# A transformer block in split fp32 on one core: w_down by seven products over pairs of column blocks

## The chip, the cores and the metric

The kernel runs on one core of one Trainium2 chip. The metric is the device time of one execution in microseconds, the median of several runs. A profile is one more execution, recorded by the hardware profiler; its span runs from the first to the last instruction.

## The reference

One layer for 256 tokens of width 2048, all in float32:

```python
h = x + concat(diff_attention(...), conformer_conv(...)) @ w_out     # from rms_norm(x) @ w_in
hn = rms_norm(h, norm2_g)
a  = hn @ w_gate          # 2048 x 5632
bu = hn @ w_up            # 2048 x 5632
y  = h + (silu(a) * bu) @ w_down    # 5632 x 2048
```

The change lies in the last line.

## The kernel before

**Split products.** A float32 product is made of three matmuls in a rounded format: each operand is cut into a hi half (rounded) and a lo half (what rounding left), and hi x hi, lo x hi and hi x lo are added up in a PSUM bank. A weight tile `raw` is loaded by SP's queue; ACT casts it to `whi`; DVE subtracts to get `wlo` (`split_chunk`, L326). For chunks with `by_dma`, ACT writes minus the hi half into `wlo` (L320) and a DMA on POOL's queue adds the weight from DRAM to it (L321), so DVE is spared.

**Chunks.** All matrix products are a list of chunks, run in order by `run_chunks`. Each chunk is loaded, rounded, split and multiplied, with leads (how many chunks ahead of the multiplication) given by the function `lead`: (5, 5, 3, 2) for load, DMA, hi and lo in the gate blocks, 2 for everything in the rest. What ends (a block's sums) runs as a generator, `start`ed at the end of a block and `resume`d twice in a chunk, so its steps land between the steps of the chunks that follow, in program order, on each engine. Engines take their instructions in that order.

**The feed-forward part.** The hidden width 5632 is cut into eleven blocks j of 512 columns of w_gate and w_up. They form three groups (`FGROUPS = (4, 4, 3)`); after each group w_down is applied to that group's columns (the w_down stage of groups 0, 1 and 2).

Blocks 1 to 10 are fast blocks: gate and up for both halves of the tokens form a 2x2 by 2x2 product, done with seven products in place of eight (Strassen's scheme in Winograd's form) on four pairs of k-tiles, and plainly on the other eight k-tiles. An "s" unit is one pair of k-tiles: ACT rounds the raw tiles `wb` to `wh` (L910), DVE makes three sums of weights `wt` (L907 to L909), ACT rounds these too (L911), DVE makes `wl` (L915 from wb, L916 from wt), and PE makes 7 products x 3 matmuls (L932 to L934), added to the banks Q1 to Q7. A "g" or "u" unit is a two: two k-tiles of gate or up, plain, 12 matmuls (L949, L950, L955). The order of the units is a string, with a capital where the lo half is made by DMA:

```python
ORDER = "sgGsgGsUUsUu"   # blocks 2 to 10
FIRST = "gugusgsUsGsU"   # block 1
PRODUCTS = ((Q1, 0, 5), (Q6, 5, 1), (Q7, 6, 2), (Q5, 4, 3), (Q2, 1, 6), (Q4, 3, 0), (Q3, 2, 4))   # bank, form of hn, form of the weights
```

A fast block is 4 x 21 + 8 x 12 = 180 matmuls of 128x512. When its last s unit is done, `products_done` copies bank Q1 on ACT and adds up the other banks on DVE; after the block's last unit, `block_done` adds the last two banks, multiplies by silu of the gate (L1013, L1015), and some chunks later `transposed` turns the result into left operands for w_down: two sets of four transposes on PE (`ps_a`, L827), each turned into `ahi` by ACT (L829) and `alo` by DVE (L831).

The w_down stage of a group has four column blocks of 512, each with 16 (12 in group 2) k-tiles x 2 token halves x 3 matmuls (L356, L357, L362), in chunks of two k-tiles: 384 matmuls (288). Groups 0 and 1 copy each result from PSUM on ACT (`part`) and add it to the output in DRAM with a DMA on POOL's queue. Group 2 fetches the sums so far over SP's queue (`fetch_sums`, L1025), adds on DVE and writes the result.

Of the kernel before, what the change touches and what calls it, by code (L numbers as in the profile page):

```python
# [18 lines left out]
P = 128  # L19
D = 2048  # L20
# [37 lines left out]
RAW_BUFS = 5  # L58
# [24 lines left out]
PRODUCTS = ((Q1, 0, 5), (Q6, 5, 1), (Q7, 6, 2), (Q5, 4, 3), (Q2, 1, 6), (Q4, 3, 0), (Q3, 2, 4))  # L83

LOAD_AHEAD, DMA_AHEAD, HI_AHEAD, LO_AHEAD = 5, 5, 3, 2

# [14 lines left out]
def tile_block(  # L101
# [9 lines left out]
    small = ctx.enter_context(tc.tile_pool(name="small", bufs=4))  # L111

    lhs = ctx.enter_context(tc.tile_pool(name="lhs", bufs=KD // 2))
# [3 lines left out]
    pre = prestack.enter_context(tc.tile_pool(name="pre", bufs=2))  # L117
    acc_ps = ctx.enter_context(tc.tile_pool(name="acc", bufs=4, space=PSUM))
# [22 lines left out]
    cols = const.tile([P, NR], F32, tag="cols", name="cols")  # L141
# [11 lines left out]
    neg_lam = const.tile([P, 1], F32, tag="neg_lam", name="neg_lam")  # L153
# [55 lines left out]

    halves = {}  # L210
# [6 lines left out]
    def lhs_two(pfx, k):  # L217
        return tuple(lhs.tile([P, 2, S], F32R, tag=f"l{x}", name=f"{pfx}{x}{k}") for x in ("hi", "lo"))
# [165 lines left out]
    def run_chunks():  # L384
# [16 lines left out]
        for t in range(n):  # L401
# [17 lines left out]
            if t in fetch_at:  # L419
                fetch_sums(fetch_at[t])  # L420
# [8 lines left out]
    rstd1 = [const.tile([P, 1], F32, tag=f"rstd1_{m}", name=f"rstd1_{m}") for m in range(NM)]  # L429
# [324 lines left out]
    ss2 = [const.tile([P, 4], F32, tag=f"ss2_{m}", name=f"ss2_{m}") for m in range(NM)]  # L754
    rstd2 = [const.tile([P, 1], F32, tag=f"rstd2_{m}", name=f"rstd2_{m}") for m in range(NM)]

    def out_done(n, ps):
# [28 lines left out]
        if n == D // N - 1:  # L786
# [8 lines left out]
            ffn["pool"] = ctx.enter_context(tc.tile_pool(name="ffn", bufs=1))  # L795
# [23 lines left out]

    def transposed(j, aa):  # L820
        for t in range(N // P // 2):
# [6 lines left out]
            hi, lo = lhs_two("a", j * (N // P) + 2 * t)  # L828
            act.copy(hi, pt)  # L829
            yield from lag(2)  # L830
            dve.tensor_tensor(lo, pt, hi.bitcast(F32), ALU.subtract)  # L831
            for i in range(2):
                actT[j * (N // P) + 2 * t + i] = (hi[:, i, :], lo[:, i, :])
            yield from lag(2 if j else 1)

    forms = {}

    def make_forms():  # L840
# [33 lines left out]
        f = fp.tile([P, 7, NS, P], F32, tag="wh", name="sums", bufs=2)  # L874
        dve.scalar_tensor_tensor(f[:, 4], a21, -1.0, a22, ALU.mult, ALU.subtract)
        dve.scalar_tensor_tensor(f[:, 5], f[:, 4], -1.0, a11, ALU.mult, ALU.subtract)
        act.copy(fhi[:, 0], a11)
        act.copy(fhi[:, 1], a12)
        act.activation(fhi[:, 3], a22, AF.Copy, scale=-1.0)
        yield  # L880
        dve.tensor_tensor(f[:, 6], a11, a21, ALU.subtract)
        dve.tensor_tensor(f[:, 2], a12, f[:, 5], ALU.subtract)
        act.copy(fhi[:, 4:7], f[:, 4:7])
        act.copy(fhi[:, 2], f[:, 2])
# [4 lines left out]
        dve.scalar_tensor_tensor(flo[:, 3], a22, -1.0, fhi[:, 3].bitcast(F32), ALU.mult, ALU.subtract)  # L889
        dve.tensor_tensor(flo[:, 2], f[:, 2], fhi[:, 2].bitcast(F32), ALU.subtract)  # L890
        yield
        dve.tensor_tensor(flo[:, 4:7], f[:, 4:7], fhi[:, 4:7].bitcast(F32), ALU.subtract)
        forms.update(hi=fhi, lo=flo)

    def load_pair(c):
        c["b"] = early.tile([P, 4, N], F32, tag="wb", name="wb")
        src = weights([(w, k, c["col"], N) for w in ("w_up", "w_gate") for k in (c["k"], c["k"] + HK)])
        sp.dma_start(out=c["b"].rearrange("p k n -> p (k n)"), in_=src)
# [26 lines left out]
    def multiply_pair(c):  # L925
        while "hi" not in forms:
            resume()
        fhi, flo, p = forms["hi"], forms["lo"], c["k"]
        for n, (q, f, w) in enumerate(c["products"]):
# [11 lines left out]
    def multiply_two(c):  # L941
        hi, lo = c["hi"], c["lo"]
        qs = (Q3, QX) if c["kind"] == "u" else (Q2, Q4)
        for i, k in enumerate(c["ks"]):
            x1, x2 = forms["plain"][k]
            for m, q in enumerate(qs):
                ms = slice(m * P, (m + 1) * P)
                ps = sum_bank(c, q)
                pe.matmul(ps, x1[:, ms], hi[:, i, :], start=i == 0 and bool(c["first"].get(q)), stop=False)  # L949
                pe.matmul(ps, x2[:, ms], hi[:, i, :], start=False, stop=False)  # L950
        resume()
        for m, q in enumerate(qs):
            ms = slice(m * P, (m + 1) * P)
            for i, k in enumerate(c["ks"]):
                pe.matmul(sum_bank(c, q), forms["plain"][k][0][:, ms], lo[:, i, :], start=False,  # L955
                          stop=i == 1 and bool(c["last"].get(q)))
# [4 lines left out]
    def fast_block(j, order, after_down):  # L961

        units, sums = [], {}
        left = dict(s=list(range(NS)), g=list(TWOS), u=list(TWOS))
        for unit in order:
            kind = unit.lower()
            what = left[kind].pop(0)
            c = dict(kind=kind, sums=sums, done=None, first={}, last={})
            if kind == "s":
                c.update(k=what, col=j * N, by_dma=False, load=load_pair, round=round_pair, split=split_pair,  # L970
                         multiply=multiply_pair, uses=[q for q, _, _ in PRODUCTS], products=PRODUCTS)
            else:
                c.update(ks=what, w="w_gate" if kind == "g" else "w_up", nk=2, width=N, cols=[(j * N, N)],
                         by_dma=unit.isupper(),
                         load=load_chunk, round=round_chunk, split=split_chunk, multiply=multiply_two,
                         uses=(Q3, QX) if kind == "u" else (Q2, Q4))
            units.append(c)
        assert not any(left.values())
        if after_down:

            units[0]["products"] = PRODUCTS[4:] + PRODUCTS[:4]
        for q in range(8):
            users = [c for c in units if q in c["uses"]]
            users[0]["first"][q] = users[-1]["last"][q] = True
        [c for c in units if c["kind"] == "s"][-1]["done"] = products_done
        units[-1].update(done=lambda sums: block_done(j, sums), prompt=True)
        chunks.extend(units)
# [3 lines left out]
    def products_done(q):  # L991
# [11 lines left out]
        act.activation(w1, w1, AF.Silu)  # L1003
        dve.tensor_tensor(u3, q[Q4], u3, ALU.add)
        act.activation(u3, u3, AF.Silu)
        halfway.update(g=(w1, u3), u=(u2, w4))

# [11 lines left out]
    so_far, fetch_at = {}, {}  # L1019

    def fetch_sums(n):
        so_far[n] = []
        for m in range(NM):
            t = ffn["pool"].tile([P, N], F32, tag=f"sum{n % 2 * NM + m}", name="so_far")
            sp.dma_start(out=t, in_=out[m * P : (m + 1) * P, n * N : (n + 1) * N])  # L1025
# [102 lines left out]
```

## Time and profile before

| | |
|---|---|
| median of 3 runs | 1081.86 us (1079.11 to 1083.89) |
| profiled execution, its own time | 1078.51 us |
| its span | 1076.7 us |
| gate blocks 1, 2, 3 | 397.8 to 526.1 us |
| w_down stage of group 0 | 526.1 to 614.1 us |
| gate blocks 4 to 7 | 614.1 to 783.2 us |
| w_down stage of group 1 | 783.2 to 871.2 us |
| gate blocks 8 to 10 | 871.2 to 997.7 us |
| w_down stage of group 2 | 997.7 to 1072.1 us |

Engines: PE is TensorE's matmul, PEld its weight load, DVE VectorE, ACT ScalarE, POOL GpSimd, SP SyncE. L12 is line 12 of the kernel. A row of instructions gives start and duration, then what was written and read; in brackets, the idle time before it and what ended it. A matmul's recorded duration overlaps the next one's, so matmuls are priced by the distance of their starts. A suffix q (SPq) is an engine's queue that issues DMAs.

### The profile page before, as it was taken

What the parts mean: (1) busy time and instruction counts of PE and PEld (TensorE: products, weight loads), DVE (VectorE), ACT (ScalarE), POOL (GpSimd) and SP (SyncE); (2) the same over time, 40 slices, a digit from 0 to 9 for tenths busy, and PEclk for the clock granted to TensorE, in tenths of its full rate; (3) what the DMA queues carried; (4) which work ended last, traced back from release to release, by engine and by line L of the source; (5) the groups of instructions that cost most, each with busy time, mean ns of one, the idle gap of its engine ahead of it and who ended that gap; (6) DMA issues with size and microseconds to landing.
All of it is one profiled execution on the core that took longest, in us unless ns stands there. A gap on an engine that the chain in (4) does not pass through costs nothing. (4 is left out here: it accounts for less than half of the span.)

```text
span 1076.7 us, 13151 instructions
## 1 busy us (share of the span) xinstructions
PE 1051.7 (98%) x4834; PEld 870.9 (81%) x4834; DVE 801.4 (74%) x979; ACT 618.0 (57%) x811; POOL 110.4 (10%) x155
## 2 busy tenths in 40 slices
PE   8999999999999999999999999999999999999798
PEld 7988888877888887788888878878888878888686
DVE  4799988899666689988644688889745477897353
ACT  6544566756756557757343667586544474765231
POOL 0130112200100100101000111010001010100000
PEclk9999999999999999999999999999999999999899
DMA  9555555344457568898476898988847799887471
GB/s 314 205 176 180 200 189 176 137 176 151 143 190 242 175 228 252 284 304 244 153 232 197 267 295 252 293 221 268 259 157 201 239 277 319 223 273 208 145 278 66
DMA packets 62781, 236.57 MB, mean 220 GB/s; under 512 B 7044, under 2 KB 8510, under 8 KB 57596
## 3 DMA queue, kind: packets, MB, share of 16 engines
q1 hardware_dynamic: 52320, 202.66, 52.1%
q0 software_dynamic: 10336, 33.04, 16.6%
q8 instruction: 38, 0.62, 0.2%
q14 instruction: 27, 0.22, 0.1%
q10 hardware_dynamic: 60, 0.03, 0.0%
HBM read 227.30 MB, written 8.39 MB: 219 GB/s over the span
## 5 line engine op out<-in xcount | busy, mean ns | idle before, releaser
L317 ACT CAST whi<-raw 128x1024 fp32r<-128x1024 f32 (+1 forms) x297 | 305.8, 1050 | 183.2 <-PE acc L357 98.1
L326 DVE TENSOR_TENSOR wlo<-raw,whi 128x1024 fp32r<-128x1024 f32 (+1 forms) x249 | 299.7, 1219 | 142.8 <-ACT whi L317 140.9
L357 PE MATMUL acc<-whi,alo 128*128 128x512 f32 x384 | 150.5, 392 | 6.6 <-DVE alo L831 6.6
L356 PE MATMUL acc<-whi,ahi 128*128 128x512 f32 x384 | 150.4, 392 | 0.0
L356 PE MATMUL acc<-whi,xhi 128*128 128x512 f32 (+1 forms) x352 | 131.0, 378 | 3.2 <-ACT xhi L223 2.4
L357 PE MATMUL acc<-whi,xlo 128*128 128x512 f32 (+1 forms) x352 | 129.5, 374 | 0.5 <-DVE xlo L224 0.4
L949 PE MATMUL q<-whi,chi 128*128 128x512 f32 x320 | 124.7, 390 | 0.0
L950 PE MATMUL q<-whi,clo 128*128 128x512 f32 x320 | 124.6, 389 | 0.0
L932 PE MATMUL q<-wh,fhi 128*128 128x512 f32 x280 | 109.7, 392 | 1.7 <-DVE alo L831 1.7
L934 PE MATMUL q<-wl,fhi 128*128 128x512 f32 x280 | 109.0, 389 | 0.0
L933 PE MATMUL q<-wh,flo 128*128 128x512 f32 x280 | 109.0, 389 | 0.0
L512 DVE SCALAR_TENSOR_TENSOR y<-upad,cw,y 128x256 f32<-128x256 f32 x240 | 103.7, 483 | 4.4 <-ACT y L505 3.9
L362 PE MATMUL acc<-wlo,ahi 128*128 128x512 f32 x384 | 103.6, 391 | 0.0
L911 ACT CAST wh<-wt 128x2048 fp32r<-128x2048 f32 x40 | 76.5, 1912 | 38.3 <-DVE wt L909 37.6
L916 DVE TENSOR_TENSOR wl<-wt,wh 128x2048 fp32r<-128x2048 f32 x40 | 91.7, 2291 | 6.6 <-ACT wh L911 5.9
L915 DVE TENSOR_TENSOR wl<-wb,wh 128x1536 fp32r<-128x1536 f32 x40 | 70.1, 1754 | 27.9 <-ACT wh L910 27.9
L357 PEld LDWEIGHTS acc<-whi,alo 128*128 128x128 f32 x384 | 72.6, 189 | 22.1 <-DVE alo L831 6.9
L362 PE MATMUL acc<-wlo,xhi 128*128 128x512 f32 (+1 forms) x352 | 88.3, 376 | 1.4 <-DVE wlo L326 1.4
L955 PE MATMUL q<-wlo,chi 128*128 128x512 f32 x320 | 86.6, 392 | 2.8 <-DMA wlo<-in_wts_dram 2.8
L356 PEld LDWEIGHTS acc<-whi,ahi 128*128 128x128 f32 x384 | 72.5, 189 | 15.3 <-ACT ahi L829 0.2
L362 PEld LDWEIGHTS acc<-wlo,ahi 128*128 128x128 f32 x384 | 71.7, 188 | 14.6
L356 PEld LDWEIGHTS acc<-whi,xhi 128*128 128x128 f32 x352 | 67.2, 191 | 14.9 <-ACT xhi L223 2.8
(197 smaller groups left out, 1487.2 us busy)
## 6 DMA issues: line engine op xcount, KB each, us to landing
raw<-in_wts_dram SPq DMA_DIRECT2D x295, 512.0 KB, 4.9
wb<-in_wts_dram SPq DMA_DIRECT2D x40, 1024.0 KB, 6.2
wlo<-in_wts_dram POOLq DMA_DIRECT2D x48, 512.0 KB, 8.3
out_dram<-part POOLq DMA_DIRECT2D x16, 256.0 KB, 5.1
out_dram<-h POOLq DMA_DIRECT2D x8, 256.0 KB, 5.9
so_far<-out_dram SPq DMA_DIRECT2D x8, 256.0 KB, 4.4
h<-in_x_dram SPq DMA_DIRECT2D x6, 256.0 KB, 7.6
out_dram<-so_far POOLq DMA_DIRECT2D x6, 256.0 KB, 3.0
```

What stands on the lines that cost most here:

```text
L317: act.copy(c["hi"], c["raw"])
L326: dve.tensor_tensor(c["lo"], c["raw"], c["hi"].bitcast(F32), ALU.subtract)
L356: pe.matmul(ps[m], xhi[:, ms], hi[:, j, :], start=c["first"] and j == 0, stop=False)
L357: pe.matmul(ps[m], xlo[:, ms], hi[:, j, :], start=False, stop=False)
L362: pe.matmul(ps[m], xhi[:, ms], lo[:, j, :], start=False, stop=c["last"] and j == nk - 1)
L512: dve.scalar_tensor_tensor(y[:, ct, :], src, wk, y[:, ct, :], ALU.mult, ALU.add)
L916: dve.tensor_tensor(c["lo"][:, :4], c["t"], c["hi"][:, :4].bitcast(F32), ALU.subtract)
L932: pe.matmul(ps, fhi[:, f, p, :], c["hi"][:, w], start=bool(first), stop=False)
L933: pe.matmul(ps, flo[:, f, p, :], c["hi"][:, w], start=False, stop=False)
L934: pe.matmul(ps, fhi[:, f, p, :], c["lo"][:, w], start=False, stop=bool(last))
L949: pe.matmul(ps, x1[:, ms], hi[:, i, :], start=i == 0 and bool(c["first"].get(q)), stop=False)
L950: pe.matmul(ps, x2[:, ms], hi[:, i, :], start=False, stop=False)
```

## The change

w_down now uses `fast_block` too. Two neighbouring column blocks take the place of up and gate; three pairs of the group's k-tiles go through the seven products, the remaining five twos (three in group 2) are plain. A block of two column blocks is 3 x 21 + 10 x 12 = 183 matmuls where there were 192, in group 2 63 + 6 x 12 = 135 where there were 144; there are two such blocks in a group.

- The three pairs of each group need seven forms of the left operand, hi and lo: `pair_forms` makes them when the tile is transposed, that is in the next gate block: two pairs in blocks 2, 5 and 9, one in 3, 6 and 10. A plain tile is treated as before.
- The bank sums are one step, all on DVE, with the copy of Q1; sums of the second column block go to DRAM (POOL's queue) as soon as the products are done, those of the first when the block is.
- PRODUCTS has another order: the first product reads a form from the second half of wl (the one made of wt).
- Leads are 5, 5, 3, 2 from the first gate block to the end. The first block after a w_down stage no longer starts with other products.
- The lo half of four of ten twos (two of six in group 2) in a w_down block is made by DMA.
- Only the last block fetches sums, on POOL's queue. RAW_BUFS is 4 instead of 5. The left operands lie in one `arena`; small tiles of the earlier stages are closed earlier.

```diff
-RAW_BUFS = 5
+RAW_BUFS = 4
-PRODUCTS = ((Q1, 0, 5), (Q6, 5, 1), (Q7, 6, 2), (Q5, 4, 3), (Q2, 1, 6), (Q4, 3, 0), (Q3, 2, 4))
+PRODUCTS = ((Q6, 5, 1), (Q7, 6, 2), (Q5, 4, 3), (Q1, 0, 5), (Q2, 1, 6), (Q4, 2, 0), (Q3, 3, 4))
+DOWN = (dict(pairs=((1, 0), (1, 1), (2, 0)), order="gsGgsGgsuUuUu"),
+        dict(pairs=((4, 0), (4, 1), (5, 0)), order="gsGgsGgsuUuUu"),
+        dict(pairs=((8, 0), (8, 1), (9, 0)), order="gsGsgsuUu"))
...
-            hi, lo = lhs_two("a", j * (N // P) + 2 * t)
-            act.copy(hi, pt)
-            yield from lag(2)
-            dve.tensor_tensor(lo, pt, hi.bitcast(F32), ALU.subtract)
...
+            if (j, t) in d["pairs"]:
+                yield from pair_forms(j, t, pt)
+            else:
+                hi, lo = d["at"][j, t]
+                act.copy(hi, pt)
+                yield from lag(2)
+                dve.tensor_tensor(lo, pt, hi.bitcast(F32), ALU.subtract)
...
+    def pair_forms(j, t, pt):
...
+        a = fp.tile([P, 2, NM, P], F32, tag="sum0", name="af")
+        act.copy(a, pt)
+        a11, a21, a12, a22 = a[:, 0, 0], a[:, 0, 1], a[:, 1, 0], a[:, 1, 1]
+        act.copy(fhi[:, :2], a[:, :, 0])
+        act.activation(fhi[:, 2], a22, AF.Copy, scale=-1.0)
+        yield
+        f = fp.tile([P, 4, P], F32, tag="sum2" if j else "sum1", name="fs")
+        dve.scalar_tensor_tensor(f[:, 1], a21, -1.0, a22, ALU.mult, ALU.subtract)
+        dve.scalar_tensor_tensor(f[:, 2], f[:, 1], -1.0, a11, ALU.mult, ALU.subtract)
+        dve.tensor_tensor(f[:, 3], a11, a21, ALU.subtract)
+        dve.tensor_tensor(f[:, 0], a12, f[:, 2], ALU.subtract)
+        act.copy(fhi[:, 3:], f)
+        yield
+        dve.tensor_tensor(flo[:, :2], a[:, :, 0], fhi[:, :2].bitcast(F32), ALU.subtract)
+        dve.scalar_tensor_tensor(flo[:, 2], a22, -1.0, fhi[:, 2].bitcast(F32), ALU.mult, ALU.subtract)
+        yield
+        dve.tensor_tensor(flo[:, 3:], f, fhi[:, 3:].bitcast(F32), ALU.subtract)
...
-        if after_down:
-
-            units[0]["products"] = PRODUCTS[4:] + PRODUCTS[:4]
...
-        act.copy(w1, q[Q1])
-        yield
+        dve.tensor_copy(w1, q[Q1])
         dve.tensor_tensor(u2, q[Q6], w1, ALU.add)
         dve.tensor_tensor(u3, q[Q7], u2, ALU.add)
-        yield
...
-            sp.dma_start(out=t, in_=out[m * P : (m + 1) * P, n * N : (n + 1) * N])
...
+    def down_products(n, q, last):
+        so_far = None
+        if last:
+            so_far = ffn["pool"].tile([P, 4, N], F32, tag="wt", name="so_far")[:, :NM]
+            pool.dma_start(out=so_far, in_=out[:, n * N : (n + 1) * N].rearrange("(m p) n -> p m n", p=P))
+        bank_sums(q)
+        for m in range(NM):
+            add_to_out(m, n + 1, halfway["g"][m])
+        yield
...
-            block("w_down", n * N, range(j0 * 4, (j0 + nb) * 4), fa, lambda ps, g=g, n=n: down_done(g, n, ps))
...
+        for n in range(0, D // N, 2):
+            down_block(g, n)
```

Where it moves instructions, shown at three places. First, DVE in gate block 5, where the two tiles of block 4 are turned into left operands, from the first tile's to the second unit of sums that follows. `alo16` and `alo18` are the lo halves of the two tiles. Before:

```order
L831 TENSOR_TENSOR alo16_5890<-ps_a_5884,ahi16_5889 128x512
L907 TENSOR_TENSOR wt_5925<-wb_5872 128x1024
L908 TENSOR_TENSOR wt_5925<-wb_5872,wt_5925 128x512
L909 TENSOR_TENSOR wt_5925<-wt_5925,wb_5872 128x512
L831 TENSOR_TENSOR alo18_5944<-ps_a_5938,ahi18_5943 128x512
L915 TENSOR_TENSOR wl_5962<-wb_5872,wh_5926 128x1536
L916 TENSOR_TENSOR wl_5962<-wt_5925,wh_5926 128x2048
```

The same place now, from the end of the first tile's forms on; `af` is the transposed tile, `fs` the four sums of forms, `lhi` and `llo` the arena's halves:

```order
L894 TENSOR_TENSOR llo_91<-fs_5890,lhi_90 128x4x128
L963 TENSOR_TENSOR wt_5927<-wb_5865 128x1024
L964 TENSOR_TENSOR wt_5927<-wb_5865,wt_5927 128x512
L965 TENSOR_TENSOR wt_5927<-wt_5927,wb_5865 128x512
L885 SCALAR_TENSOR_TENSOR fs_5961<-af_5951 128x128
L886 SCALAR_TENSOR_TENSOR fs_5961<-fs_5961,af_5951 128x128
L887 TENSOR_TENSOR fs_5961<-af_5951 128x128
L888 TENSOR_TENSOR fs_5961<-af_5951,fs_5961 128x128
L891 TENSOR_TENSOR llo_91<-af_5951,lhi_90 128x2x128
L892 SCALAR_TENSOR_TENSOR llo_91<-af_5951,lhi_90 128x128
L971 TENSOR_TENSOR wl_5972<-wb_5865,wh_5928 128x1536
L972 TENSOR_TENSOR wl_5972<-wt_5927,wh_5928 128x2048
```

Where one subtraction stood between wt and wl there are six smaller operations.

Second, DVE at the start of the w_down stage of group 2, behind the last gate block's products (L1015, now L1108). Before:

```order
L1015 TENSOR_TENSOR sum3_8334<-sum3_8334,sum2_8333 128x512
L326 TENSOR_TENSOR wlo_8370<-raw_8292,whi_8346 128x1024
L326 TENSOR_TENSOR wlo_8388<-raw_8319,whi_8386 128x1024
L326 TENSOR_TENSOR wlo_8404<-raw_8344,whi_8402 128x1024
L326 TENSOR_TENSOR wlo_8430<-raw_8426,whi_8428 128x1024
L831 TENSOR_TENSOR alo40_8420<-ps_a_8414,ahi40_8419 128x512
```

Now:

```order
L1108 TENSOR_TENSOR sum3_8387<-sum3_8387,sum2_8386 128x512
L963 TENSOR_TENSOR wt_8424<-wb_8367 128x1024
L964 TENSOR_TENSOR wt_8424<-wb_8367,wt_8424 128x512
L965 TENSOR_TENSOR wt_8424<-wt_8424,wb_8367 128x512
L971 TENSOR_TENSOR wl_8445<-wb_8367,wh_8425 128x1536
L972 TENSOR_TENSOR wl_8445<-wt_8424,wh_8425 128x2048
L342 TENSOR_TENSOR wlo_8484<-raw_8404,whi_8450 128x1024
L963 TENSOR_TENSOR wt_8493<-wb_8422 128x1024
L964 TENSOR_TENSOR wt_8493<-wb_8422,wt_8493 128x512
L965 TENSOR_TENSOR wt_8493<-wt_8493,wb_8422 128x512
L869 TENSOR_TENSOR llo_91<-ps_a_8474,lhi_90 128x512
```

The lo half of the last block's first transposed tile stands behind two units' sums of weights.

Third, PE at that place: who needs that lo half. Before, it is the first matmul with `alo40`, in the fifth chunk of the w_down stage (the transposes stand in its third):

```order
L362 MATMUL acc_8372<-wlo_8388,ahi38_8171 128x512 x2
L362 MATMUL acc_8373<-wlo_8388,ahi38_8171 128x512 x2
L356 MATMUL acc_8372<-whi_8402,ahi40_8419 128x512
L357 MATMUL acc_8372<-whi_8402,alo40_8420 128x512
L356 MATMUL acc_8373<-whi_8402,ahi40_8419 128x512
```

Now it is the first L1007 row here, in the third unit, a two, behind the transposes and the last of the seven products:

```order
L862 MATMUL ps_a_8474<-ident_85,sum1_8385 128x128
L862 MATMUL ps_a_8474<-ident_85,sum3_8387 128x128
L862 MATMUL ps_a_8474<-ident_85,sum1_8385 128x128
L862 MATMUL ps_a_8474<-ident_85,sum3_8387 128x128
L988 MATMUL q6_8480<-wh_8370,lhi_90 128x512
L989 MATMUL q6_8480<-wh_8370,llo_91 128x512
L990 MATMUL q6_8480<-wl_8401,lhi_90 128x512
L1006 MATMUL q4_8431<-whi_8337,lhi_90 128x512
L1007 MATMUL q4_8431<-whi_8337,llo_91 128x512
```

Between the transposes and the first reader of that lo half stood 17 matmuls; now four do.

More of the change, by code (lines that the diff above doesn't have):

```diff
@@ L208, in rsqrt_mean @@
         pool.tensor_tensor(dst, t[:, :k], neghalf[:, :k], ALU.pow)
+    slot = [0]
     halves = {}
@@ new lines, in down_done @@
+    def down_done(n, q, last):
+        while "added" not in halfway:
+            yield
+        halfway.pop("added")
+        halfway.pop("g")
+        u = halfway.pop("u")
+        parts = 2 if last else 1
+        w = N // parts
+        for m, i in enumerate((Q3, QX)):
+            for part in range(parts):
+                ws = slice(part * w, (part + 1) * w)
+                dve.tensor_tensor(u[m][:, ws], q[i][:, ws], u[m][:, ws], ALU.add)
+                if last:
+                    sp.dma_start(out=out[m * P : (m + 1) * P, n * N + part * w : n * N + (part + 1) * w], in_=u[m][:, ws])
+            if last and m == 0:
+                yield
+        if not last:
+            for m in range(NM):
+                add_to_out(m, n, u[m])
```

208 lines of the change are left out of this document (120 added, 88 removed).

## The prediction, made before the result was known

> **What bounds the kernel now.** I read the page's first lines, then a table of the span by stage, then the list of what the engines waited for, and last the rows around the waits of TensorE (PE). The page says that PE has hardly any time off:
>
> ```profile
> span 1076.7 us, 13151 instructions
> ## 1 busy us (share of the span) xinstructions
> PE 1051.7 (98%) x4834; PEld 870.9 (81%) x4834; DVE 801.4 (74%) x979; ACT 618.0 (57%) x811; POOL 110.4 (10%) x155
> ```
>
> The table gives, for each stretch, its length, then the busy time of PE, PEld, DVE, ACT and POOL, the granted PE clock, the share of time that the DMA engines were busy, and GB/s. The rows are gate block 2; then the w_down stage of group 0, gate blocks 4, 5, 6, 7; then gate block 8; then the w_down stage of group 2.
>
> ```profile
> 441.60:484.30 42.70, 41.96 (x190) 34.48 (x189) 38.17 (x39) 28.34 (x27) 4.31 (x5) 1.00 0.93 284
> ...
> 526.10:614.10 88.00, 88.00 (x394) 72.85 (x393) 47.97 (x44) 37.44 (x41) 5.24 (x6) 1.00 0.71 219
> 614.10:656.80 42.70, 41.03 (x181) 33.67 (x180) 31.08 (x27) 28.53 (x26) 6.98 (x8) 1.00 1.00 291
> 656.80:698.70 41.90, 41.90 (x189) 34.49 (x188) 35.99 (x34) 28.27 (x26) 4.31 (x5) 1.00 0.86 256
> 698.70:741.40 42.70, 41.98 (x189) 34.49 (x188) 38.05 (x39) 28.26 (x26) 4.35 (x5) 1.00 0.89 269
> 741.40:783.20 41.80, 41.80 (x190) 34.57 (x189) 32.37 (x34) 27.14 (x27) 3.47 (x4) 1.00 0.74 219
> ...
> 871.20:913.40 42.20, 41.06 (x181) 33.70 (x180) 30.56 (x26) 28.59 (x26) 6.94 (x8) 1.00 1.00 288
> ...
> 997.70:1072.10 74.40, 67.76 (x297) 55.58 (x295) 33.78 (x36) 22.38 (x23) 3.31 (x6) 0.95 0.48 170
> ```
>
> The w_down stage of group 0 is PE from end to end: 88.0 us for 384 matmuls and 8 transposes. With 0.8 us for the transposes, a matmul costs 87.2/384 = 0.227 us. A clean gate block (block 7) is 180 matmuls, 40.8 us, and two sets of transposes: 41.8. So PE sets the time, and the rest must be on time for it. This is where it was not, in the whole FFN:
>
> ```profile
> PE acc L357 <- DVE alo L831: 6.6, 1, 6.6
> PE q L955 <- DMA wlo<-in_wts_dram: 2.8, 2, 1.7
> PE ps_a L827 <- DVE alo L831: 1.9, 3, 0.7
> PE q L932 <- DVE alo L831: 1.7, 1, 1.7
> ```
>
> The columns are the total, the times and the longest wait. The 6.6 us are in the w_down stage of group 2 (67.76 of 74.40 busy); the 2.8 us stand in the first gate blocks behind a w_down stage.
>
> **Fewer matmuls.** A new w_down block has 183 matmuls instead of 192 (groups 0 and 1), or 135 instead of 144. Nine fewer in six blocks are 54 x 0.227 = 12.2 us, all on the path. This is the whole gain that the change is sure of.
>
> **One set of leads.** At the first gate block after w_down the leads jump from 2 to 5, the loads crowd (share 1.00 in block 4), and a lo half made by DMA is late. Block 4 holds no transposes, so its 42.7 us are 1.9 above 40.8; block 8, the same place in group 2, took 42.2 and lost 1.4, 1.1 of it by the second of the L955 waits (2.8 - 1.7). With leads of 5, 5, 3, 2 throughout, there is no jump: -3.3. What could be late next are the same lo halves inside w_down, below.
>
> **Pair forms inside the gate blocks.** Nine pairs of transposed k-tiles, two each in gate blocks 2, 5, 9 and one each in 3, 6, 10, get seven forms instead of one hi and one lo. Old price: one 128x512 subtraction on DVE. New price on DVE: four operations of 128 columns, one of 256, one of 128 and one of 512. The nearest rows for 128 columns on DVE and on ACT (name, shape, count, busy time, mean ns):
>
> ```profile
> L692 DVE SCALAR_TENSOR_TENSOR wt<-pr,r,p 128x128 f32<-128x128 f32 x4 | 1.4, 347 | 0.0
> L616 ACT ACTIVATE qn<-acc,fq 128x128 f32<-128x128 f32 x8 | 2.3, 385 | 0.4 <-POOL fq L612 0.4
> ```
>
> Consecutive starts on DVE lie about 0.09 us closer than the durations say (a 0.69 operation every 0.60). Five operations at 0.26, one of 256 columns at some 0.33 between the two, and one at 0.60 are 2.2, less 0.6 for the old one: 1.6 us of DVE per pair. ACT has 0.5 (copy of 512), 0.35, 0.3 and 0.5 in place of 0.5: some 1.1 more. Is that hidden? Block 5 has the rows, where the third unit of seven products waits for its weights (DVE, then ACT, then PE; start, duration):
>
> ```profile
> 673.94 0.69 DVE L831 TENSOR_TENSOR alo<-ps_a,ahi 128x512 fp32r<-128x512 f32 x1 [2.45 <-ACT ahi L829]
> 674.55 1.75 DVE L915 TENSOR_TENSOR wl<-wb,wh 128x1536 fp32r<-128x1536 f32 x1
> 676.21 2.29 DVE L916 TENSOR_TENSOR wl<-wt,wh 128x2048 fp32r<-128x2048 f32 x1
> ```
>
> ```profile
> 671.52 1.91 ACT L911 CAST wh<-wt 128x2048 fp32r<-128x2048 f32 x1
> 673.33 0.58 ACT L829 CAST ahi<-ps_a 128x512 fp32r<-128x512 f32 x1
> ```
>
> ```profile
> 678.78 0.39 PE L934 MATMUL q<-wl,fhi 128*128 128x512 f32 x1
> ```
>
> The weights' lo is done at 678.50 and PE reads it at 678.78: 0.3 us of slack. In the changed order the first pair's forms stand ahead of this unit's sums wt, which end 1.6 to 2.2 us later (the 0.6 is the bank copy that DVE takes from ACT). ACT rounds wt, 1.9, and only then copies the second pair, 0.5; then DVE makes four sums, 1.2, and two lo forms, 0.7, before wl, 3.9. In the row wt is done when ACT begins with it, at 671.52; 671.5 + 1.9 + 1.9 + 0.5 + 1.2 + 0.7 + 3.9 is 681.6, and PE wants it at 678.78. And the products now begin with one that reads wl's second half, so the order of reading gives nothing back. The stall is 2.2 to 2.8, since part of the bank copy falls into DVE's wait ahead of the sums; I take 2.3 in blocks 5 and 9. Block 2 has DVE busy 38.17 of 42.70 where block 5 has 35.99, so its unit starts later: 2.3 + 1.3 = 3.6. A block with one pair has only the first part, 1.6 plus what the copy adds less the slack: 1.4 in blocks 3, 6 and 10. Together 2 x 2.3 + 3.6 + 3 x 1.4 = 12.4. The waits for ps_a (1.9) lie in blocks with pairs and go under in these: +10.5. The low end is 0, if DVE's idle time (5.9 of 41.9 in block 5) lies where it is needed; the high end 15, with 2.8 and 1.9 for the doubles and singles.
>
> **The third group's start.** Today's 6.6 us wait there comes from SP: the fetch of the sums so far is queued ahead of six loads.
>
> ```profile
> SPq L1025 <- DVE sum L1015: 13.5, 1, 13.5
> SPq L1025 <- PE ps_a L827: 11.6, 1, 11.6
> ```
>
> ```profile
> 1019.24 0.80 PE L357 MATMUL acc<-whi,alo 128*128 128x512 f32 x1 [6.64 <-DVE alo L831]
> 1019.84 0.63 PE L356 MATMUL acc<-whi,ahi 128*128 128x512 f32 x1
> 1020.26 0.63 PE L357 MATMUL acc<-whi,alo 128*128 128x512 f32 x1
> ```
>
> Behind that wait, matmuls came every 0.43 us for eight of them: 1.6 more, so 8.2 in all. The change moves the fetch to the last block and to POOL. But the lo of that last block's transposes now has other work before it on DVE; its prices:
>
> ```profile
> 660.22 1.22 DVE L907 TENSOR_TENSOR wt<-wb 128x1024 f32<-128x1024 f32 x1
> ...
> 662.81 1.75 DVE L915 TENSOR_TENSOR wl<-wb,wh 128x1536 fp32r<-128x1536 f32 x1
> 664.87 2.29 DVE L916 TENSOR_TENSOR wl<-wt,wh 128x2048 fp32r<-128x2048 f32 x1 [0.31 <-ACT wh L911]
> 667.08 1.22 DVE L326 TENSOR_TENSOR wlo<-raw,whi 128x1024 fp32r<-128x1024 f32 x1
> ```
>
> wt takes 2.6, wl with its wait 4.3, wlo 1.1. Counted from the first down matmul: seven bank sums of 0.6 start 24 matmuls (5.4) before it and end 1.2 before it; wl 3.9; the block's last adds and products 2.4; wt 2.6, wl 4.3, wlo 1.1, wt 2.6, and the lo, 0.6, ends at 15 to 16. PE wants it in its third unit, after 12 + 21 + 1 matmuls and four transposes: at 8.1. So a wait of some 7 us stays, for another reason, with its slow matmuls: 8.7 for 8.2, +0.5. If the order gives way the gain is 8.2; if the next wt also waits for its load, it is some 3 worse.
>
> **The clock after a wait.** Behind a wait of 1.67 us (block 4) four matmuls took 1.00 us, nearly full speed:
>
> ```profile
> 625.19 1.17 PE L955 MATMUL q<-wlo,chi 128*128 128x512 f32 x4 [1.67 <-DMA wlo<-in_wts_dram]
> 626.19 0.39 PE L932 MATMUL q<-wh,fhi 128*128 128x512 f32 x1
> ```
>
> Between 1.67 us (nothing) and 6.64 us (1.6) I give the new waits together 0.8, mainly block 2's. The Trainium skill's "TensorE: Matmul & The Clock Gate", Part 1, says that after an idle window of about 3.4 us the array runs at half rate until about 3.4 us of work have passed. The trace agrees in kind (0.43 against 0.227). By that rule the wait of block 2 alone would add up to 1.7, and two waits in one window more; the sum would be 1 us higher.
>
> **Down blocks otherwise.** DVE and ACT have room there (47.97 and 37.44 of 88). The second block of a group waits for wl of its unit by 0 to 0.3, and group 2's unit by 0.75: +1.0. Bank sums all on DVE take 4.2 and end 3 us before the next block's products need the banks: 0. Four buffers for raw instead of five: 0, since SP's queue is held by the two wb buffers already. The adds of sums to DRAM now stand between lo halves on POOL's queue and hold those behind them until DVE has the sums; lo halves are issued five units, some 15 us, ahead, so 0. The tail stays.
>
> **DMA in w_down.** Twenty more lo halves are made by adding DMA. Shares in the old stage of group 0 (packets, MB, share of 16 engines; q0 is POOL's queue):
>
> ```profile
> q1 hardware_dynamic: 4409, 17.67, 58.0%
> q0 software_dynamic: 864, 1.57, 12.8%
> ```
>
> A new block of 183 x 0.227 = 41.5 us moves three tiles of 1 MB and ten of 0.5 MB of weights (8.4 MB), four lo halves (2.1) and four sums of 128x512 (1.05): 11.5 MB. Block 4 moved 291 GB/s x 42.7 = 12.4 MB with its engines busy throughout; at that rate 11.5 MB take 39.5 us. It fits with 5% to spare, so I take +1.0 for lateness in the six blocks, with 0 below and 25 above (rival b). The Trainium skill, "DMA: Bandwidth & Descriptors", Specifications, gives about 358 GB/s for one core's HBM traffic; by it the block would need 32 us and the term would be 0. The trace's 291 at share 1.00 lies below that, and I go by the trace.
>
> **Sum.** -12.2 - 3.3 + 10.5 + 0.5 + 0.8 + 1.0 + 1.0 = -1.7 us on a span of 1076.7. The profiled execution took 1078.51, so it would be 1076.8; the median of the runs shown is 3.35 above it: 1080.
>
> **Rivals.** (a) The forms are hidden. For it: DVE idles 11 to 23% and ACT a third of every such block, and the planner of the order may place the forms where there is air. Against: slack of 0.3 us in the row. Then -1.7 - 10.5 = -12.2, 1070; if the third group's wait of 8.2 goes too, 1061. (b) DMA becomes the bound in w_down: slower. In the old stage the weights cost 58.0% of 88 us for 17.67 MB, 2.9 us per MB, and q0 7.2 us per MB. At those prices a block needs 8.4 x 2.9 + 3.15 x 7.2 = 47 us against 41.5 of PE, 5.5 us in each of four blocks and less in the last two: up to +25; if lo halves cost less than sums in DRAM, about half: 1092. It decides once a block needs over 41.5. Against it stand block 4's 12.4 MB. (c) Everything as summed, but the doubles clog DVE for a whole block and the wait passes to the next one: three blocks at +3, 1089.
>
> **How the numbers follow.** My sum, 0.40; (a) 0.36; (b) 0.13; (c) 0.11. A measurement of this kernel tells about 0.5% (5.4 us) from no change. The sum lies within that, with a little spill to both sides; (a) is faster, (b) and (c) slower: faster 0.38, same 0.38, slower 0.24. The range runs from (a)'s middle, 1064, to (b)'s near end, 1091; the likeliest case's own is 1074 to 1087.
>
> **What would show it.** Right: PE waits in the first products of the third unit in blocks 5, 9 and 2 for DVE's wl, 2 to 4 us each; a wait of some 7 us for DVE's lo in the first down block of group 2; no DMA wait in blocks 4 and 8; w_down stages of 83 us in groups 0 and 1. Wrong: gate blocks with pairs at 42 us (a), or w_down stages over 85 us with PE waiting for wlo by DMA at share 1.00 (b).

## The result and the profile after

The changed kernel takes 1096.94 us (median of 4 runs, 1095.98 to 1097.6) where the one before takes 1080.48: a ratio of 1.0148, 95% interval 1.0118 to 1.0179. It is 16 us slower; the forecast was 1080, between 1064 and 1091.

The page's first lines, and the list of what PE waited for over the whole program:

```profile
span 1094.2 us, 13181 instructions
## 1 busy us (share of the span) xinstructions
PE 1051.0 (96%) x4780; PEld 865.5 (79%) x4780; DVE 902.5 (82%) x1124; ACT 654.9 (60%) x831; POOL 130.5 (12%) x176
```

```profile
PE q L990 <- DVE wl L972: 18.6, 11, 3.5
PE q L1007 <- DVE llo L869: 4.4, 1, 4.4
PE q L1006 <- ACT lhi L867: 3.3, 1, 3.3
PE acc L372 <- ACT lhi L239: 2.9, 2, 2.5
PE q L988 <- DVE llo L869: 2.4, 1, 2.4
```

PE has 54 fewer matmuls but is busy just as long, 1051.0 against 1051.7: some of those left ran slower. And one wait is new, most of it in the gate blocks: 18.6 us in 11 pieces for wl, the lo half of the weights of a unit of seven products. The table by stage, in the columns of the table before (gate blocks 1 to 3, w_down of group 0, gate blocks 4 to 7, w_down of group 1, gate blocks 8 to 10, then the two blocks of w_down of group 2):

```profile
399.10:445.20 46.10, 43.67 (x190) 35.64 (x189) 41.14 (x36) 28.77 (x24) 3.54 (x4) 0.96 0.89 297
445.20:492.50 47.30, 42.66 (x190) 34.34 (x189) 42.29 (x53) 30.30 (x32) 4.30 (x5) 1.00 0.81 241
492.50:538.50 46.00, 43.63 (x189) 35.59 (x188) 37.44 (x43) 30.21 (x31) 4.34 (x5) 0.96 0.79 218
538.50:623.90 85.40, 84.21 (x376) 69.32 (x374) 70.10 (x67) 50.38 (x45) 12.26 (x14) 1.00 0.91 265
623.90:664.70 40.80, 40.80 (x182) 33.78 (x180) 33.01 (x30) 23.14 (x19) 6.12 (x7) 1.00 1.01 309
664.70:710.80 46.10, 42.41 (x190) 34.43 (x189) 40.88 (x50) 30.05 (x31) 4.30 (x5) 1.00 0.81 231
710.80:757.10 46.30, 43.64 (x189) 35.54 (x188) 40.77 (x45) 30.60 (x31) 4.32 (x5) 0.96 0.83 247
757.10:798.90 41.80, 41.80 (x190) 34.59 (x189) 34.71 (x35) 27.85 (x26) 4.33 (x5) 1.00 0.84 240
798.90:884.20 85.30, 84.19 (x376) 69.34 (x375) 69.99 (x67) 49.49 (x44) 12.21 (x14) 1.00 0.92 265
884.20:925.00 40.80, 40.80 (x182) 33.78 (x181) 33.49 (x31) 23.90 (x21) 6.10 (x7) 1.00 1.00 308
925.00:972.20 47.20, 43.69 (x189) 35.55 (x188) 42.27 (x51) 31.91 (x34) 4.32 (x5) 0.96 0.80 234
972.20:1015.10 42.90, 42.09 (x190) 34.50 (x189) 34.98 (x41) 27.67 (x28) 4.35 (x5) 1.00 0.77 209
1015.10:1058.20 43.10, 34.87 (x145) 27.67 (x144) 33.44 (x33) 18.64 (x17) 3.47 (x4) 0.88 0.62 183
1058.20:1090.10 31.90, 31.35 (x136) 24.87 (x134) 26.75 (x29) 11.99 (x10) 5.14 (x6) 1.00 0.59 149
```

The two stages of 88.0 us are 85.4 and 85.3. Gate blocks 4 and 8 are at PE's own 40.8. The six gate blocks in which pair forms are made (2, 3, 5, 6, 9, 10) took 42.7, 41.8, 41.9, 42.7, 42.5 and 41.8 and now take 47.3, 46.0, 46.1, 46.3, 47.2 and 42.9: 22.4 us more. Group 2's w_down takes 75.0 where it took 74.4, with 18 matmuls fewer. In four of the rows the granted clock is 0.96, in one 0.88.

Block 5 shows how one wait comes about: DVE, then ACT, then PE.

```profile
681.24 0.69 DVE L965 TENSOR_TENSOR wt<-wt,wb 128x512 f32<-128x512 f32 x1
685.21 0.29 DVE L885 SCALAR_TENSOR_TENSOR fs<-af 128x128 f32<-128x128 f32 x1 [3.28 <-ACT af L879]
...
686.69 1.75 DVE L971 TENSOR_TENSOR wl<-wb,wh 128x1536 fp32r<-128x1536 f32 x1
688.36 2.28 DVE L972 TENSOR_TENSOR wl<-wt,wh 128x2048 fp32r<-128x2048 f32 x1
```

```profile
677.10 0.62 ACT L889 CAST lhi<-fs 128x512 fp32r<-128x512 f32 x1 [1.22 <-DVE fs L888]
...
681.43 1.47 ACT L966 CAST wh<-wb 128x1536 fp32r<-128x1536 f32 x1
682.80 1.91 ACT L967 CAST wh<-wt 128x2048 fp32r<-128x2048 f32 x1
684.61 0.58 ACT L879 COPY af<-ps_a 128x512 f32<-128x512 f32 x1
```

```profile
690.70 0.50 PE L990 MATMUL q<-wl,fhi 128*128 128x512 f32 x1 [3.51 <-DVE wl L972]
```

wl, whose first half could have begun at 682.9 when ACT had finished the first part of wh, stands on DVE behind the second tile's forms. These wait 3.28 us for ACT's copy `af`, and ACT had been busy without a gap since 677.10. The row at 677.10 is ACT's rounding of the first tile's sums: it had waited 1.22 us for DVE and stands ahead of four more casts and of both parts of wh. So ACT waits for DVE, and then DVE for ACT.

### The profile page after: what moved, and what is told of

It reads as the page before. It is cut to its first block, busy times and chain, and to the rows that moved or that the text cites. A ratio compares the mean times of both kernels' runs of the same rounds, so it can differ in the third digit from the quotient of the medians.

```text
span 1094.2 us, 13181 instructions
## 1 busy us (share of the span) xinstructions
PE 1051.0 (96%) x4780; PEld 865.5 (79%) x4780; DVE 902.5 (82%) x1124; ACT 654.9 (60%) x831; POOL 130.5 (12%) x176
## 4 chain that ended last, share of the span: by engine, by line
PE 34%; DVE 16%; ACT 8%; issue 6%; DMA 2%; POOL 0%; SPq 0%; DVEq 0%; ACTq 0%
PE q L1007 7%; PE q L1006 7%; PE q L1011 6%; PE q L990 5%; PE q L988 5%; PE q L989 5%; DVE wl L972 4%; ACT wh L967 3%; DMA raw<-in_wts_dram 2%; DVE wt L963 2%; ACT whi L333 2%; DVE wlo L342 2%; ACT wlo L336 2%; DVE wl L971 1%; DVE wt L964 1%
## 5 line engine op out<-in xcount | busy, mean ns | idle before, releaser
L342 DVE TENSOR_TENSOR wlo<-raw,whi 128x1024 fp32r<-128x1024 f32 (+1 forms) x193 | 233.4, 1218 | 74.6 <-ACT whi L333 74.4
L372 PE MATMUL acc<-whi,lhi 128*128 128x512 f32 (+1 forms) x448 | 168.3, 380 | 3.2 <-ACT lhi L239 2.9
L373 PE MATMUL acc<-whi,llo 128*128 128x512 f32 (+1 forms) x448 | 166.5, 376 | 0.5 <-DVE llo L240 0.4
L337 POOL DMA_DIRECT2D wlo<-in_wts_dram x68 | 61.4, 903 | 553.1 <-ACT wlo L336 468.1
L1007 PE MATMUL q<-whi,clo 128*128 128x512 f32 x320 | 124.6, 389 | 0.0
L378 PE MATMUL acc<-wlo,lhi 128*128 128x512 f32 (+1 forms) x448 | 114.4, 380 | 1.7 <-DVE wlo L342 1.7
L372 PEld LDWEIGHTS acc<-whi,lhi 128*128 128x128 f32 x448 | 84.9, 189 | 18.9 <-ACT lhi L239 3.3
L373 PEld LDWEIGHTS acc<-whi,llo 128*128 128x128 f32 x448 | 84.9, 190 | 15.7 <-DVE llo L240 0.9
L378 PEld LDWEIGHTS acc<-wlo,lhi 128*128 128x128 f32 x448 | 79.6, 188 | 17.3 <-DVE wlo L342 3.0
L966 ACT CAST wh<-wb 128x1536 fp32r<-128x1536 f32 x58 | 85.1, 1468 | 3.9 <-issue 2.5
L336 ACT ACTIVATE wlo<-raw 128x1024 fp32r<-128x1024 f32 x68 | 71.7, 1054 | 0.0
```

The lines of the kernel that those rows point to most:

```text
L342: dve.tensor_tensor(c["lo"], c["raw"], c["hi"].bitcast(F32), ALU.subtract)
L372: pe.matmul(ps[m], xhi[:, ms], hi[:, j, :], start=c["first"] and j == 0, stop=False)
L373: pe.matmul(ps[m], xlo[:, ms], hi[:, j, :], start=False, stop=False)
L378: pe.matmul(ps[m], xhi[:, ms], lo[:, j, :], start=False, stop=c["last"] and j == nk - 1)
L1007: pe.matmul(ps, plain[i][1][:, ms], hi[:, i, :], start=False, stop=False)
```

## Experiments

The theory (A): wl is late because a tile's work stands ahead of it on DVE and waits for ACT there, and PE's idle time then costs half-clock matmuls too. Its rivals are named with the runs.

**The forms' work taken away.**

In `pair_forms` (cut at the dots):

```diff
-        a = fp.tile([P, 2, NM, P], F32, tag="sum0", name="af")
-        act.copy(a, pt)
...
-        dve.tensor_tensor(flo[:, 3:], f, fhi[:, 3:].bitcast(F32), ALU.subtract)
+        act.copy(fhi[:, :4], pt.rearrange("p a b -> p (a b)").rearrange("p (f c) -> p f c", f=4))
+        yield from lag(2)
+        dve.tensor_tensor(flo[:, :4], pt.rearrange("p a b -> p (a b)").rearrange("p (f c) -> p f c", f=4), fhi[:, :4].bitcast(F32), ALU.subtract)
...
+            f = f if c["sides"][0][0] != "w_down" else f % 4
```

> The nine pair tiles are treated like plain ones: one rounding on ACT and one subtraction on DVE give four of the seven forms, the other three products of w_down read these again. It leaves out the sums of forms, so w_down's result is another one; PE's work is the same. Theory A (the extra work for the forms makes the third unit's weights late in gate blocks 2, 3, 5, 6, 9, 10, and a part of the waits is followed by half-clock matmuls): these six blocks, 277 us in the changed kernel's profile, fall to about 254, time 1074 to 1078. Rival B (the new order of the seven products, whose first reads the half of wl that is done last): the waits stay, 1092 or more. Rival C (bank sums with their copy on DVE push everything back): the waits stay, 1092 or more.

1076.63 us, ratio 0.9965 [0.9949, 0.9981]. The six blocks take 44.6, 41.9, 41.9, 42.9, 43.4 and 42.4 us, 257 together, where 254 was forecast; PE's waits for wl in the whole FFN fall from 18.6 us to 2.8. So the 20 us come with the forms' work; the order of the products and the bank sums, unchanged here, do not cost them by themselves.

**The order of the products.**

```diff
-PRODUCTS = ((Q6, 5, 1), (Q7, 6, 2), (Q5, 4, 3), (Q1, 0, 5), (Q2, 1, 6), (Q4, 2, 0), (Q3, 3, 4))
+PRODUCTS = ((Q1, 0, 5), (Q6, 5, 1), (Q7, 6, 2), (Q5, 4, 3), (Q2, 1, 6), (Q4, 2, 0), (Q3, 3, 4))
```

> Only the order of the seven products goes back (Q1 first, which reads the half of wl that is done first). Theory A: in a stalled unit the second product still needs the second half, so each wait ends at most 0.7 us earlier: six waits, -2 to -4 us, more only if a wait falls under what drops the clock: 1090 to 1096. Rival B: the waits of 2.4 to 3.5 go, 1080 or less.

1097.04 us, ratio 1.0149 [1.0128, 1.0169]: no difference from the changed kernel, so theory A's 1090 to 1096 is missed by a little. The wait of block 5 splits in two, 1.17 for wl's first half and 1.24 for its second. Over the six blocks the waits for wl are 13.1 us where they were 17.5, somewhat more than the 2 to 4 us of theory A, but the total did not follow: blocks 2 and 10 and the w_down stage of group 0 were 1.9, 2.3 and 2.8 us longer in this profile. Rival B, which had the waits gone, falls.

**The bank copy.**

```diff
-        dve.tensor_copy(w1, q[Q1])
+        act.copy(w1, q[Q1])
+        yield
         dve.tensor_tensor(u2, q[Q6], w1, ALU.add)
         dve.tensor_tensor(u3, q[Q7], u2, ALU.add)
+        yield
...
-        bank_sums(q)
+        yield from bank_sums(q)
```

> The copy of bank Q1 goes back to ACT, with the two steps between the sums that were there before. Theory A: DVE is 0.6 us a block earlier, ACT 0.6 later, and the wait hangs on both: within 3 us of the changed kernel, 1094 to 1100. Rival C: -15, about 1082.

1107.43 us, ratio 1.0246 [1.0227, 1.0265]: 10 us slower, outside what either theory said. Rival C falls, but the sums made early, in one step and on one engine, turn out to be needed; which of the two counts, this run does not separate. A w_down block begins with a g unit, whose banks the sums of the block before still hold:

```profile
PE q L990 <- DVE wl L972: 14.9, 8, 3.5
PE q L1006 <- DVE sum L1093: 14.4, 3, 5.3
```

Three waits of 4.2 to 5.3 us, one at each change from gate blocks to w_down, that the changed kernel doesn't have (the second row). The first row shows the old trouble still there.

**One step later.**

```diff
-        yield
+        yield from lag(2)
         f = fp.tile([P, 4, P], F32, tag="sum2" if j else "sum1", name="fs")
```

> One step more before the sums of a pair's forms, nothing else: in blocks 2, 5 and 9 the second pair's six operations on DVE stand behind wl of the third unit instead of ahead of it, the work is the same. Theory A (order on DVE: wl waits for a pair tile that itself waits for ACT): the waits of 3.5 us in blocks 2, 5, 9 fall to under 1.5, and blocks 3, 6, 10 (one pair) stay: -6 to -9, 1088 to 1091. Rival D (it is the sum of the work on DVE that is too much, wherever it stands): no change, 1095 to 1098.

1078.09 us, ratio 0.9973 [0.9961, 0.9985]: 19 us faster than the changed kernel with the same work, more than expected, since blocks 3, 6 and 10 gained as well (42.6, 42.3, 42.1). There the second tile is a plain one, and its lo half, made in the same generator, also stepped behind wl. The step moves one thing more than was expected: ACT's rounding of a tile's sums (L889) comes later too, and in block 5 it waits 0.45 us for DVE where it waited 1.22. Rival D, as a matter of the sum of the work, falls. PE's waits for wl in the whole FFN, 18.6 us before the step:

```profile
PE q L990 <- DVE wl L972: 4.8, 9, 1.1
```

Block 5 of this kernel on DVE, from the end of wt on:

```profile
674.39 0.68 DVE L894 TENSOR_TENSOR llo<-fs,lhi 128x512 fp32r<-128x512 f32 x1
675.32 1.76 DVE L971 TENSOR_TENSOR wl<-wb,wh 128x1536 fp32r<-128x1536 f32 x1 [0.24 <-ACT wh L966]
677.12 2.29 DVE L972 TENSOR_TENSOR wl<-wt,wh 128x2048 fp32r<-128x2048 f32 x1
679.33 0.28 DVE L885 SCALAR_TENSOR_TENSOR fs<-af 128x128 f32<-128x128 f32 x1
```

Now wl starts 0.9 us after the first row, and the second tile's forms follow it; what DVE lost waiting for ACT, 3.28, is 0.24. The stretch rows of blocks 5 and 6 and of w_down's second block of group 1:

```profile
657.80:700.10 42.30, 42.07 (x190) 34.50 (x189) 40.57 (x49) 30.06 (x31) 4.30 (x5) 1.00 0.87 259
700.10:742.40 42.30, 42.09 (x190) 34.52 (x189) 38.37 (x42) 28.81 (x28) 4.32 (x5) 1.00 0.86 260
830.10:871.60 41.50, 41.50 (x184) 34.27 (x183) 35.18 (x33) 26.21 (x24) 7.01 (x8) 1.00 1.00 289
```

DVE is busy 40.57 of 42.30 us and PE hardly waits.

**The forms' price at the later place.**

In `pair_forms` (cut at the dots), with the products of w_down as in the first experiment:

```diff
-        a = fp.tile([P, 2, NM, P], F32, tag="sum0", name="af")
-        act.copy(a, pt)
...
-        dve.tensor_tensor(flo[:, 3:], f, fhi[:, 3:].bitcast(F32), ALU.subtract)
+        act.copy(fhi[:, :4], pt.rearrange("p a b -> p (a b)").rearrange("p (f c) -> p f c", f=4))
+        yield from lag(2)
+        dve.tensor_tensor(flo[:, :4], pt.rearrange("p a b -> p (a b)").rearrange("p (f c) -> p f c", f=4), fhi[:, :4].bitcast(F32), ALU.subtract)
+        yield from lag(2)
...
```

> The kernel with one step more ahead of the forms, and the forms at the price of a plain tile (one rounding, one subtraction at the later place; the three other forms are not made, so w_down's result is another one). Theory A: at that place the forms' work is hidden, so within 2 us of the kernel with the forms, 1076 to 1080. Rival D (the sum of DVE's and ACT's work costs wherever it stands): 1072 or less.

1075.05 us, ratio 0.9941 [0.9923, 0.9959]; with the forms it was 0.9973 [0.9961, 0.9985]. The intervals just miss each other. By the ratios the difference is some 3.5 us, more than the 2 of theory A and less than rival D's 6; in the two profiles the six blocks with forms differ by 1.7 us. So the forms' work is mostly hidden at that place, not wholly, and neither theory's number held.

**The start of group 2's w_down.**

Besides the later step in `pair_forms`:

```diff
                 act.copy(hi, pt)
-                yield from lag(2)
+                yield from lag(1 if j in (0, 3, 7, 10) else 2)
```

> The kernel with one step more ahead of the forms (the last experiment), and besides the lo half of plain tiles one step earlier for blocks 0, 3, 7 and 10, whose tiles are wanted at once. In block 10's case it goes on DVE ahead of a lo half and three sums of weights, 3.7 us. Theory A (the start of each w_down stage waits by the place of the lo half on DVE): group 2's first block 43.2 to about 39, the first blocks of groups 0 and 1 a microsecond less, block 1 the same or up to 3 less: 1069 to 1074. Rival E (DVE as a whole is behind at that place, so wl, now behind it, is late by as much): 1077 to 1079.

1077.58 us, ratio 0.9969 [0.9953, 0.9985]. The place does what theory A says: group 2's first block goes from 43.4 to 39.3 us, and PE's second wait from 4.43 to 1.0:

```profile
1011.80 0.50 PE L1006 MATMUL q<-whi,lhi 128*128 128x512 f32 x1 [3.28 <-ACT lhi L867]
1013.30 0.68 PE L1007 MATMUL q<-whi,llo 128*128 128x512 f32 x1 [1.00 <-DVE llo L869]
```

The total did not follow: blocks 1, 3 and 10 were 1.3, 0.7 and 0.9 us longer and the first blocks of groups 0 and 1 did not gain. The trace puts this down to DVE, as rival E does: in block 1 the wait of 2.56 us for the lo half is gone, but PE waits there 1.22 and 0.81 for wl and 1.87 at the block's end for a bank sum, and at the ends of blocks 3 and 10 it waits 0.78 and 0.59 for bank sums.

**The leads alone, on the kernel before.**

```diff
+    first_fast = next(i for i, c in enumerate(chunks) if "kind" in c)
...
-                      if "kind" in chunks[t] else (AHEAD,) * 4)
+                      if t >= first_fast else (AHEAD,) * 4)
```

> The kernel before with one part of the change alone: leads of 5, 5, 3, 2 from the first fast block on, in w_down too. Theory of the prediction: blocks 4 and 8 fall from 42.7 and 42.2 to about 40.8, nothing else moves: 1077 to 1078. Rival: more loads in flight in w_down delay those of the sums in group 2 and the wait of 6.6 there grows: 1081 or more.

> The kernel before with leads alone, once more, beside the one with later lo halves on the same chip: 1068 to 1071.

1069.51 us, ratio 0.9885 [0.9846, 0.9924], and again 1067.57, ratio 0.9854 [0.9831, 0.9876]. That is 12 and 15 us under the kernel before, about four times the 3.3 that the prediction gave the leads, and the second is a little under its forecast. The rows of blocks 4 and 8 and of group 2's w_down:

```profile
617.40:658.20 40.80, 40.80 (x182) 33.78 (x181) 32.56 (x28) 26.79 (x24) 6.12 (x7) 1.00 1.02 312
873.70:914.50 40.80, 40.80 (x182) 33.78 (x181) 33.09 (x29) 27.19 (x25) 6.10 (x7) 1.00 1.02 314
998.30:1065.20 66.90, 66.67 (x297) 54.56 (x295) 34.09 (x36) 22.46 (x23) 3.31 (x6) 1.00 0.50 181
```

The 3.3 us of blocks 4 and 8 came as forecast. Another 7.5 are group 2's w_down, 74.4 to 66.9. The rest of the gain is not found at one place: in the first run's profile blocks 1, 2 and 7 were even longer, by 1.7, 1.2 and 1.7 us. In group 2, more loads of weights are issued on SP's queue ahead of the fetch of the sums, twelve since the last gate block's `wb` where it was nine (before, then with the leads):

```profile
963.61 22.02 SPq L313 DMA_DIRECT2D raw<-in_wts_dram  x9
999.41 12.27 SPq L1025 DMA_DIRECT2D so_far<-out_dram  x2
```

```profile
964.51 38.01 SPq L313 DMA_DIRECT2D raw<-in_wts_dram  x12
1002.88 9.44 SPq L1025 DMA_DIRECT2D so_far<-out_dram  x2
```

Between the last of these loads and the next one behind the fetch lay 26 us before and 10 us now, and PE no longer waits for what follows from it. This fix for the wait of 6.6 us was in the change, unseen in the prediction, but in the changed kernel another wait stands at that place.

**The later lo half on the kernel before.**

```diff
             act.copy(hi, pt)
-            yield from lag(2)
+            yield from lag(3)
```

> The kernel before, with its lo halves of tiles one step later, so that they stand behind wl of the third unit as in the mended kernel. Theory A (before there was no wait for wl at that place, so there is nothing to win): 1079 to 1082; waits for ps_a of a microsecond may come or go. Rival F (the step is good by itself, whatever the forms): 1076 or less.

1082.88 us, ratio 1.0013 [0.9994, 1.0032]: nothing to win, as theory A has it (a microsecond above its range). In the parts, blocks 2, 6 and 9 fell to 41.8, but block 1 rose to 50.3 and group 2's w_down by 2: a tile that is wanted at once must not step back. That gave the next version.

**Leads, and later lo halves where they can wait.**

Besides the leads of the experiment before last:

```diff
-            yield from lag(2)
+            yield from lag(2 if j in (0, 3, 7, 10) else 3)
```

> The kernel before with the leads of 5, 5, 3, 2 throughout, and the lo halves of tiles one step later except in blocks 0, 3, 7, 10 (whose tiles are wanted soon, and where a later lo half cost 6.5 us in block 1 and 2 in group 2). Theory A: blocks 2, 6 and 7 of the kernel with leads alone (43.9, 42.2, 43.5) fall to 41.8, where the later lo halves had them: 3 to 4 us under it, 1065 to 1067. Rival G (such differences of 2 us come and go with the clock's windows from run to run): the same as with leads alone, 1068 to 1070.

1065.76 us, ratio 0.9843 [0.982, 0.9867], beside 0.9854 [0.9831, 0.9876] for leads alone on the same chip: the fastest version here, though the intervals overlap and the 1.8 us between them are not settled. Blocks 6 and 7 are at 41.8, as theory A said; but block 7 was at 41.8 in the second run with leads alone as well, as rival G said.

**Group 2's w_down undone.**

```diff
-        dict(pairs=((8, 0), (8, 1), (9, 0)), order="gsGsgsuUu"))
+        dict(pairs=(), order=""))
...
+            block("w_down", n * N, range(j0 * 4, (j0 + nb) * 4), fa, lambda ps, n=n: plain_done(n, ps))
...
```

> The kernel with one step more ahead of the forms, and group 2's w_down undone: plain, four column blocks, leads of 5, 5, 3, 2, sums fetched over SP's queue; no pair forms in blocks 9 and 10. Theory A: the 18 matmuls saved in group 2 (4.1 us) cost more than they bring, since its first block waits 8 us for a lo half: the stage goes from 74.9 to about 67, 1068 to 1071. Rival H (the wait comes with the place behind the gate blocks, whatever w_down is): the stage takes 75 or more, 1078 to 1082.

1071.12 us, ratio 0.989 [0.9867, 0.9913], at the upper end of theory A; with the seven products in group 2 it was 0.9973. The stage takes 66.9 us instead of 75.3:

```profile
997.10:1064.00 66.90, 66.67 (x297) 54.53 (x295) 34.06 (x36) 22.41 (x23) 3.30 (x6) 1.00 0.52 187
```

Rival H falls. With 18 matmuls more the stage is 8 us shorter: the waits that the seven products bring at that place cost more than the matmuls they save.

## Why the prediction was wrong

By stage, the span grew by 17.5 us: the six blocks with forms +22.4, block 1 +2.3, the start of the FFN +1.3, group 2's w_down +0.6, the w_down stages of groups 0 and 1 -5.3, blocks 4 and 8 -3.3, and 0.5 less behind the last stage. The forecast for the span was -1.7.

**Fewer matmuls, -12.2: right as a price, not wholly collected.** Each second block of w_down in groups 0 and 1 takes 41.5 us, 183 x 0.227. The first ones take 43.8 with their transposes, 1.5 more than their matmuls, of which 1.2 and 1.1 are a wait for the bank of the transposes (`ps_a`), which DVE's lo half of the tile before frees late. The sum had nothing for the first blocks, so the stages that were to take 83 us took 85.4 and 85.3.

**Leads, -3.3: right in its place, too small as a part.** Blocks 4 and 8 are at 40.8. That the same leads would end the 6.6 us wait in group 2 was missed; it had been read as a matter of the fetch's queue alone.

**Pair forms, +10.5: the step that failed.** The kind of wait was forecast, with block, unit and engine: PE waits for wl in the third unit. The sizes were not, and neither was the path that set them. Waits for wl were 3.53, 3.51 and 3.51 us in blocks 2, 5 and 9 against 2.3 taken (3.6 in block 2, which had another of 1.06), and 2.37 and 2.66 in blocks 3 and 6 against 1.4; only block 10, with 0.81, was under it. Block 5 shows the path, on the clock of the rows of before (block 5 begins 7.9 us later in the profile after). The prediction let ACT begin to round wt when DVE had summed it, at 673.4. It began at 674.9, and not because of wt, for it followed the first part of wh without a gap: ACT itself was late, since its rounding of the first tile's sums waited 1.22 us for DVE ahead of four casts and wh. ACT's extra 1.1 us had been priced, but left out of the chain. The second tile's forms took 1.5 on DVE, a little less than the 1.9 of the sum, so wl ended at 682.7 where the chain had 681.6. The wait of DVE for ACT, into which a part of the extra work was to fall, was no slack: it grew from 2.45 to 3.28. All waits for wl in the six blocks are 17.5 us, less 1.9 for ps_a: 15.5 where 10.5 stood.

**The clock after a wait, +0.8: mis-sized too.** Three of these waits (in blocks 3, 6 and 9) were followed by seven or eight matmuls at 0.43 us, up to 1.6 us each, and so was one in block 1. Block 2's wait, for which the term was mainly meant, was followed by none. In block 6 PE goes on at 735.41, after the wait of 2.66 us, and 1.6 us later the slow ones begin:

```profile
736.99 0.63 PE L990 MATMUL q<-wl,fhi 128*128 128x512 f32 x1
737.41 0.63 PE L988 MATMUL q<-wh,fhi 128*128 128x512 f32 x1
737.84 0.63 PE L989 MATMUL q<-wh,flo 128*128 128x512 f32 x1
738.27 0.63 PE L990 MATMUL q<-wl,fhi 128*128 128x512 f32 x1
```

The bounds were a wait of 1.67 us (nothing) and one of 6.64 (1.6 us); the new waits of 2.4 to 3.5 lay between and should have been priced each at up to 1.6, not all together at half of one. With 15.5 of waits and 3 x 1.6 of clock, 20.3 of the 22.4 us are named; what the remaining 2 us are was not followed up.

**Group 2's start, +0.5: the wait was right, its price was not.** PE waits 3.28 for ACT's lhi and 4.42 for DVE's llo, 7.7 together, against some 7 forecast for DVE's llo alone; some ten slow matmuls lie behind the second wait (granted clock 0.88 in that block), and 0.5 for wl ahead of the first. The stage is 4.2 us over 74.4 - 4.1 + 0.5.

**DMA, +1.0, and rival (b): nothing.** DMA shares are 0.91 and 0.92 in w_down and no wait of PE there ends with a DMA. The estimate of 39.5 us for a block from block 4's rate agrees: 0.91 of the mean block's 42.7 is 38.9.

**Not in the sum:** block 1 is 2.3 us longer (its wait for llo is 2.43 where it was 1.71, and slow matmuls follow), and the FFN starts 1.3 us later. Starts in the profiles of the other kernels lie between 397.3 and 399.9, so the latter is about as large as the scatter. Rival (a), hidden forms, is nearly what one step in the program's order gives; as the change was written it was false. Rival (c), 1089, was nearer in time than the sum, but by another way: in blocks 3 and 6 PE has no wait of half a microsecond before the third unit, so nothing passed on from the blocks with two pairs.

## What to carry to other kernels

Before adding work to an engine that is 85 to 90% busy, as DVE was in these blocks, find which instruction behind it another engine is waiting for, and put the new work behind that one; here one step was worth 19 us. An idle stretch of an engine that waits for a third engine is no cover for new work if the same change gives that third engine more to do. Try each part of a change alone: the leads were worth 12 to 15 us, and no version with the fewer matmuls, which the change was built on, was faster than the leads alone.

## What the runs showed of the hardware

Whether a wait of PE is followed by half-clock matmuls is not set by its length alone. In the changed kernel's gate blocks, waits of 2.37, 2.43 and 2.66 us were each followed by seven or eight matmuls at 0.43 us; of three waits of 3.51 to 3.53, one was and two were not. The slow stretch began 0.3 to 1.6 us after the wait's end and lasted 3.0 to 3.4 us. In all the profiles of this case, from block 1 on, 14 of 22 waits between 1.8 and 3.6 us were followed by six or more such matmuls (leaving out those at group 2's start, behind which PE waits again after one matmul), and so were all eleven of 4.1 us and more; of the waits between 1.2 and 1.8 us only two of 1.23 were, each soon behind another wait. The Trainium skill's "TensorE: Matmul & The Clock Gate", Part 1, describes a free-running window of 3.4 us in which activity is judged, which fits both the chance and the varying delay; that less than one full window of idle time (2.37 us) is enough is what these traces add to it.
